# A planner's costs recalibrated, and the 64 sample rows stacked on TensorE

## The chip, the core and the metric

One core of a Trainium2 chip runs the whole program. The metric is device time in microseconds (us), the median of several executions. The kernel writes its instructions from Python; each engine (TensorE or PE, VectorE or DVE, ScalarE or ACT, GpSimd or POOL, and SP, which issues the DMAs) runs its own queue in order, and semaphores tie the queues together.

## The reference

One layer of a streaming encoder, applied to a prompt of 2048 rows and to a sample of 64 rows that continues a stream with 4096 past positions:

```python
h = rmsnorm(x, norm_g) @ w_in                     # 1024 -> 6144 columns
qa, ka, va, za, qb, kb, vb, zb, ga, gb = split(h)
# branch A: 4 heads, two softmaxes each over 64-wide halves of q and k, ALiBi, chunk-causal
a = softmax(s[0]) - lam * softmax(s[1]);  oa = a @ v
# branch B: chunkwise retention with a decaying state, 4 heads
oa = rmsnorm(oa, subln_g) * 0.2 * silu(za);  ob = rmsnorm(ob) * silu(zb)
y  = x + (sigmoid(ga) * (oa @ w_o_diff) + sigmoid(gb) * (ob @ w_o_ret)) @ w_out
```

All of it is float32. The sample's attention reads a cache of 4096 keys and values besides its own 64. The keys, values and retention states are outputs too.

## The kernel before

**Three products for one.** Most matmul operands are split into a high and a low part (`xh`, `xl` for the normalised input, `wh`, `wl` for a weight, a type that TensorE takes in one pass), and a product is the sum of high*high, high*low and low*high: three matmuls into one PSUM tile. ScalarE makes the high part by a cast, and VectorE or GpSimd makes the low part by a subtraction.

**Three streams of work.** `w_stream` is the input projection, in two halves of the prompt; the sample rides with the first half. `natural` and `opening` put x rows on the output's partitions (q, k, v), in tiles of 128 rows, and the ninth tile has the sample's 64 rows; `transposed` puts weight columns on the partitions instead. `z_stream` is attention and retention (`qk_block`, `softmax`, `at_pv`, `sample_attn`, `sample_pv`, `ret_block`). `out_stream` is the two output projections (`m_tile`, then `y_tile` for each 128 rows). `mm_group` issues the three matmuls for each of 8 chunks of 128 input columns.

**What sets the order.** Every task is a Python generator. The planner keeps one modelled clock per engine: `P`, `A`, `V` and `G` advance that of PE, ACT, DVE and POOL by an estimated cost and return when the result should be ready; `ld` and `st` do so for DMAs. A task yields the time it waits for, and the loop runs the first task in order of priority whose time is not after the modelled PE clock. The instructions of PE, ACT and DVE then stand in their queues in the order in which the Python code issued them; the order on SP and POOL is set by the framework. So these costs change no instruction, but they do change what stands ahead of what:

```python
def A(self, n, ready=0.0, extra=0.0):
    self.act = max(self.act, ready) + 0.84 * n + 165 + extra
    return self.act + LAT
```

**Places named later.** A projection result waits in an `mm` PSUM tile (two of them) until ScalarE copies it to an `ev` tile (three). `fin_qk` normalises q and k and transposes them on PE (`tp<-ident,raw`), `ret_block` does that for retention (`tp<-ident,rru`); both go through `rsqrt_small`, three VectorE operations on a handful of columns (`sm_t`, `sm_y`). `sample_attn` runs eight exponentials per head, and then `sample_pv` brings the two 64-row softmaxes together by DMAs across partitions (`both`, `s_num`, `s_den`). Weights are split by `wh<-ws` (ACT) and `wl<-ws,wh` (POOL). Line numbers in the profile of before are those of this listing.

Of the kernel before, what the change touches and what calls it, by code (L numbers as in the profile page):

```python
# [16 lines left out]
T = 2048  # L17
# [19 lines left out]
LAT = 250.0  # L37
DMA_LAT = 2600.0
# [22 lines left out]
class Hybrid:  # L61
# [78 lines left out]
    st = ld  # L140
# [26 lines left out]
    def consts(self):  # L167
        nc, i = self.nc, self.i
        cp = self.cp

        def c(name, shape, dt=F32):
            return cp.tile(shape, dt, tag=name, name=name)

        yield lambda: len(self.xt_ready) > 8
        self.fold = c("fold", [128, 64])
# [36 lines left out]
        nc.vector.tensor_scalar_add(lam, lam, 0.2)  # L212
        self.nlam = c("nlam", [128, 1])
        nc.vector.tensor_scalar_mul(self.nlam, lam, -1.0)
        self.lsam = c("lsam", [128, 1])
        nc.vector.memset(self.lsam[0:64, :], 1.0)
        nc.vector.tensor_copy(self.lsam[64:128, :], self.nlam[64:128, :])
        for _ in range(9):
            t = self.V(1)
        self.A(2)  # L220
        self.give("row", t)

    def rsqrt_small(self, ms, n, ready):
# [12 lines left out]
        for _ in range(3):  # L236
            self.tr = self.V(20, self.act)
# [86 lines left out]
    def norm_log(self, j):  # L324
        nc = self.nc
        ss, ms, y, t = self.xin[j][9:]
        nc.scalar.activation(y, ss, AF.Ln, scale=1.0 / D, bias=self.epst[:y.shape[0]])
        nc.scalar.activation(y, y, AF.Exp, scale=-0.5)
        self.A(1, 0, 40)
        self.xin[j].append(self.A(1, 0, 40))  # L330

    def norm_mean(self, j):
        ss, ms, y, t = self.xin[j][9:13]
        self.nc.vector.tensor_scalar(ms, ss, 1.0 / D, EPS, op0=ALU.mult, op1=ALU.add)
        self.V(1, t)

    def norm_root(self, j):
# [6 lines left out]
        for _ in range(3):  # L344
            self.V(20, t2)
# [23 lines left out]
    def x_tile(self, j, wait=True, mid=None):  # L369
# [6 lines left out]
        for q in range(2):  # L376
# [14 lines left out]
            self.give(tag, t2)  # L391
            if q == 0 and mid:
                yield from mid()
# [97 lines left out]
    def mm_group(self, ps, n, us, wsl, x, wfirst, last, between=None):  # L491
        nc = self.nc
        seg, xsl = x
        for c in range(KC):
# [3 lines left out]
            ops = ((a, xh), (a, xl), (b, xh)) if wfirst else ((xh, a), (xh, b), (xl, a))  # L498
            for i, (p, q) in enumerate(ops):
# [10 lines left out]
    def opening(self, fin):  # L510
# [5 lines left out]
        self.x_alloc(1)  # L516
        us, low = [], []
# [46 lines left out]
        for j in range(1, 9):  # L564
# [15 lines left out]
            ps = self.psum("mm")  # L580
# [3 lines left out]
            self.spawn(fin(ps[:r], r, 1, 128 * j if j < 8 else T, self.pe + LAT), 0, "w")  # L584
            yield self.pe

    def natural(self, half, fin, fresh=False, wide=False):
# [6 lines left out]
        for j0 in range(0, len(tiles), per):  # L594
# [3 lines left out]
            for u, (src, r, seg, col) in enumerate(group):  # L598
                if fresh:
                    yield lambda: len(self.xt_ready) > j0 + u  # L600
                    yield self.xt_ready[j0 + u]
                yield from self.mm_group(ps[:r, n * u:n * u + n], n, us, slice(0, n),
# [4 lines left out]
            self.spawn(fin(ps[:r, :n * len(group)], r, len(group), t0, self.pe + LAT), 0, "w")  # L607
            yield self.pe

# [6 lines left out]
    def fin_qk(self, which, g, nh=2):  # L616
# [4 lines left out]
        def fin(ps, r, nu, t0, t):  # L621
# [16 lines left out]
            self.give("mm", max(t1, t2))  # L638
# [10 lines left out]
            t = self.V(8)  # L649
# [3 lines left out]
            t = self.V(n)  # L653
# [42 lines left out]
    def fin_va(self, g, nh=2):  # L696
# [4 lines left out]
        def fin(ps, r, nu, t0, t):  # L701
# [13 lines left out]
            self.give("mm", max(t2, t3))  # L715
# [17 lines left out]
    def fin_vb(self, g):  # L733
# [3 lines left out]
        def fin(ps, r, nu, t0, t):  # L737
# [5 lines left out]
            self.give("mm", t)  # L743
# [50 lines left out]
    def rms_t(self, ps, n, gain, t, tag, tmp=None):  # L794
# [35 lines left out]
        self.A(n, t)  # L830
# [14 lines left out]
        else:  # L845
            yield t
            nc.vector.scalar_tensor_tensor(out=o, in0=o, scalar=gain, in1=y, op0=ALU.mult, op1=ALU.mult)
            t = self.V(n, t)
# [134 lines left out]
    def softmax(self, st, nk, b, pair):  # L983
# [4 lines left out]
        for units, mx, t in st:  # L988
# [11 lines left out]
        for c in range(2):  # L1000
            lsum = ls[c][:, 0:1]
            if len(rows[0]) > 1:
                lsum = sp.tile([128, 1], F32, tag="a_ls", name="a_ls")
                nc.vector.tensor_add(lsum, ls[c][:, 0:1], ls[c][:, 1:2])
                self.V(1, t)
            nc.vector.reciprocal(w[:, c:c + 1], lsum)
            self.V(1, t)
        nc.vector.tensor_mul(w[:, 1:2], w[:, 1:2], self.nlam)
        t = self.V(1, t)
        yield t  # L1010
        for k, (u0, u1) in enumerate(zip(rows[0], rows[1])):
            n = u0.shape[1]
            nc.scalar.activation(u1, u1, AF.Identity, scale=w[:, 1:2])  # L1013
            t1 = self.A(n, t, 90)
# [3 lines left out]
            t2 = self.V(n, t1)  # L1018
# [73 lines left out]
    def sample_attn(self):  # L1092
# [9 lines left out]
        for h in range(4):  # L1102
# [42 lines left out]
            for m in range(9):  # L1145
# [12 lines left out]
                if m < 8:  # L1158
# [3 lines left out]
                    t = self.V(512, t)  # L1162
# [19 lines left out]
            self.A(64, t, 220)  # L1182
            te = []
            for m in range(8):
                u = units[m // 2][:, (m % 2) * 512:(m % 2) * 512 + 512]
                nc.scalar.activation(u, u, AF.Exp, bias=mx[:, m:m + 1], scale=-1.0, accum_out=lp[:, m:m + 1])
                te.append(self.A(512, t, 220))
            self.spawn(self.sample_pv(h, units, both, tail, te, lp, oall), 2, "z")
# [4 lines left out]
        for h in range(4):  # L1193
            nc.tensor.matmul(fp[:, 64 * h:64 * h + 64], oall[:, 128 * h:128 * h + 128], self.fold,
# [29 lines left out]
    def v_split(self):  # L1224

        nc = self.nc
        for m in 4 * [*range(9)]:
# [11 lines left out]
            t = self.V(128 * nt, t)  # L1239
# [3 lines left out]
    def sample_pv(self, h, units, both, tail, te, lp, oall):  # L1243
# [7 lines left out]
        l, num, den = (sp.tile([128, 1], F32, tag=k, name=k, bufs=3) for k in ("s_l", "s_num", "s_den"))  # L1251
        nc.vector.tensor_reduce(l, lp[:, :9], axis=AX.X, op=ALU.add)
        nc.vector.tensor_copy(num[lo], l[lo])
        nc.vector.tensor_copy(den[up], l[up])
# [3 lines left out]
        self.ld(num[up], l[lo], 1 << 12)  # L1258
        t = self.ld(den[lo], l[up], 1 << 12)
        tt = sp.tile([64, 64], F32, tag="s_tt", name="s_tt", bufs=2)  # L1260
        self.ld(tt, tail[up], 1 << 14)
        for k in range(2):
            self.ld(both[k][lo], units[k][up], 1 << 18)
            t = self.ld(both[k][up], units[2 + k][lo], 1 << 18)
        yield t + 600
        nc.vector.reciprocal(den, den)
        nc.vector.scalar_tensor_tensor(out=den, in0=num, scalar=den, in1=self.nlam, op0=ALU.mult, op1=ALU.mult)
        nc.vector.reciprocal(num, num)
        for _ in range(3):
            self.V(1, t)  # L1270
        tb = []
        for k in range(2):
# [3 lines left out]
            self.V(1024)  # L1276
            nc.vector.scalar_tensor_tensor(out=b[up], in0=units[2 + k][up], scalar=den[up], in1=b[up],
                                           op0=ALU.mult, op1=ALU.add)
            tb.append(self.V(1024))
            self.give("row", tb[-1], 2)  # L1280
            yield self.pe
# [70 lines left out]
    def ret_block(self, k, t0, r, first):  # L1352
# [90 lines left out]
        t = self.V(8)  # L1443
# [3 lines left out]
        t = self.V(512, t2)  # L1447
# [47 lines left out]
    def split_fin(self, tag, h, l, s, t, on_pool, slot, key):  # L1495
# [8 lines left out]
        else:  # L1504
            yield t
            nc.vector.tensor_sub(l, s, h.bitcast(F32))
            t = self.V(n, t)
# [62 lines left out]
    def og_fin(self, on, z, t, og):  # L1570
# [9 lines left out]
        t = self.V(GW, t)  # L1580
# [10 lines left out]
        t = self.V(GW, t)  # L1591
# [3 lines left out]
    def gate(self, n, pair, tag):  # L1595
# [4 lines left out]
        for br in range(2):  # L1600
            self.nc.scalar.activation(pair[br], pair[br], AF.Sigmoid, bias=self.bg[:, br, ct:ct + 1])
            t = self.A(GW, t, 90)
# [38 lines left out]
    def m_fin(self, g, ct, pss):  # L1641
# [25 lines left out]
        for d, m in zip(self.ms, (h, l)):  # L1667
            nc.vector.tensor_copy(d[:, ct, 8 * g:8 * g + 8], m[:, 256:GW])
            t2 = self.V(8)
        self.msn.append(t2)  # L1670

    def y_tile(self, g, sel, r, x, y):
# [3 lines left out]
        for nh in range(2):  # L1676
            nsl = slice(512 * nh, 512 * nh + 512)
            yield from self.take("xt")
            xt = self.sb(pb, [128, 512], "xt", "oxt")[:r]
            tx = self.ld(xt, x[:, nsl], 2048 * r)  # L1680
            yield from self.take("at")
            run.append((nsl, xt, tx, self.psum("at")[:r]))
        first = 8 if sel is None else 7
        order = [(c, k) for k in range(2) for c in range(first)] + [(c, k) for c in range(first, 8) for k in range(2)]
        for ct, nh in order:
            nsl, xt, tx, ps = run[nh]
            yield lambda: len(self.wout) > ct and nh in self.wout[ct][2] and len(self.mq[g]) > ct
            h, l, t = self.mq[g][ct]
            if sel is None:
                yield lambda: len(self.msn) == 64  # L1690
                t = max(t, self.msn[-1])
                h, l = self.ms[0][:, ct, :], self.ms[1][:, ct, :]
            else:
                h, l = sel(h), sel(l)
            wh, wl, tw = self.wout[ct]
            if max(t, tw[nh]) > self.pe:
                yield max(t, tw[nh])
            nc.tensor.matmul(ps, h, wh[:, nsl], start=ct == 0, stop=False)  # L1698
            nc.tensor.matmul(ps, h, wl[:, nsl], start=False, stop=False)  # L1699
            nc.tensor.matmul(ps, l, wh[:, nsl], start=False, stop=ct == 7)  # L1700
            for _ in range(3):
                t = self.P(512)
            yield self.pe
            if ct == 7:
                self.spawn(self.y_fin(ps, xt, y[:, nsl], r, max(t, tx)), 0)
# [13 lines left out]
    def out_stream(self):  # L1719
# [4 lines left out]
        for g in range(8):  # L1724
# [3 lines left out]
            for tt in range(2):  # L1728
                t0 = 256 * g + 128 * tt
# [4 lines left out]
        yield from self.y_tile(7, None, 64, self.i["x_sample"][0], self.o["y_sample"][0])  # L1734

    def w_stream(self):
# [54 lines left out]
        self.ms = [self.z4.tile([128, 8, 64], F32R, tag=f"ms{j}", name=f"ms{j}") for j in range(2)]  # L1791
# [87 lines left out]
def const_arrays():  # L1879
    c = {}  # L1880
    c["c_ident"] = np.eye(128, dtype=np.float32)
    c["c_fold"] = np.concatenate([np.eye(64), np.eye(64)]).astype(np.float32)
# [49 lines left out]
```

## Time and profile before

| | |
|---|---|
| median of three executions | 1988.08 us (1986.14 to 1988.54) |
| profiled execution | 1990.07 us, of which its span is 1988.3 us |
| granted TensorE clock | 0.999 |
| busy: PE, PE weight load | 1963.8 us (99%), 1754.7 us (88%) |
| busy: DVE, ACT, POOL | 1057.2 us (53%), 991.0 us (50%), 417.3 us (21%) |
| DMA | 285.21 MB, mean 143 GB/s |

The busy time of PE counts every moment in which a matmul is under way. Matmuls are pipelined, so what one costs in a row of equals is the distance between two starts, which the timeline shows, and not its own duration.

### The profile page before, as it was taken

The numbers are of one execution on the slowest core, as the hardware profiler recorded it, in microseconds if no ns is written. First come the engines' busy times: TensorE is split into PE (matmuls) and PEld (weight loads), VectorE is DVE, ScalarE is ACT, GpSimd is POOL, SyncE is SP. The second block draws the span as 40 slices with busy tenths as digits, with TensorE's granted clock in tenths as the row PEclk, the third lists the DMA queues.
The fourth block names the chain that finished last, engine by engine and source line by source line (L and its number), as shares of the span: only waits on it lengthen the run. The fifth ranks groups of instructions, "written<-read, shape, count | busy, mean of one in ns | idle before, by whom it ended". The sixth has DMA issues, their size and how long they took to land.

```text
span 1988.3 us, 34106 instructions
## 1 busy us (share of the span) xinstructions
PE 1963.8 (99%) x12206; PEld 1754.7 (88%) x12206; DVE 1057.2 (53%) x2786; ACT 991.0 (50%) x2185; POOL 417.3 (21%) x383
## 2 busy tenths in 40 slices
PE   9999999999999999999999999999999999999999
PEld 7778989998998989999998888888888888889997
DVE  6453665446565326547756656525644356444432
ACT  6432666655454436436757656635744544333330
POOL 2310121212121221221111111211122434222210
PEclk9999999999999999999999999999999999999999
DMA  7646553335665756664352342652233666444431
GB/s 245 200 143 177 138 157 118 117 87 152 174 174 152 174 151 196 200 187 137 102 153 81 109 137 62 175 146 85 70 98 114 202 219 206 141 130 148 131 93 53
DMA packets 332508, 285.21 MB, mean 143 GB/s; under 512 B 65905, under 2 KB 297329, under 8 KB 332338
## 3 DMA queue, kind: packets, MB, share of 16 engines
q1 hardware_dynamic: 332338, 283.03, 48.5%
q8 instruction: 96, 1.57, 0.3%
q14 instruction: 74, 0.61, 0.1%
HBM read 187.19 MB, written 91.49 MB: 140 GB/s over the span
## 4 chain that ended last, share of the span: by engine, by line
PE 64%; DVE 2%; DMA 2%; ACT 1%; issue 0%; POOL 0%; SPq 0%; POOLq 0%; ACTq 0%; DVEq 0%
PE mm L500 31%; PE at L1698 3%; PE at L1699 3%; PE at L1700 3%; PE s L956 2%; PE s L957 2%; PE at L1063 2%; PE mm L1630 2%; PE s L1632 2%; PE mm L1631 2%; PE mm L1632 2%; PE s L1631 2%; PE s L1630 2%; PE pv L1043 1%; PE pv L1042 1%; PE pv L1041 1%
## 5 line engine op out<-in xcount | busy, mean ns | idle before, releaser
L500 PE MATMUL mm<-xh,wh 128*128 128x512 f32 (+2 forms) x1280 | 459.3, 359 | 2.8 <-ACT ev L770 2.8
L500 PE MATMUL mm<-xh,wl 128*128 128x512 f32 (+2 forms) x1280 | 452.4, 353 | 0.0
L500 PE MATMUL mm<-xl,wh 128*128 128x512 f32 (+2 forms) x1280 | 451.8, 353 | 0.0
L472 POOL TENSOR_TENSOR wl<-ws,wh 128x512 fp32r<-128x512 f32 x189 | 258.6, 1381 | 867.2 <-ACT wh L462 605.5
L500 PE MATMUL mm<-wh,xh 128*128 128x256 f32 (+3 forms) x864 | 273.5, 317 | 0.3 <-DVE tlo L713 0.3
L500 PEld LDWEIGHTS mm<-xh,wh 128*128 128x128 f32 x1280 | 241.4, 189 | 32.4 <-ACT ev L770 3.3
L500 PEld LDWEIGHTS mm<-xh,wl 128*128 128x128 f32 x1280 | 241.1, 188 | 31.9 <-POOL wl L472 0.4
L500 PE MATMUL mm<-wh,xl 128*128 128x256 f32 (+3 forms) x864 | 267.9, 310 | 0.1
L500 PE MATMUL mm<-wl,xh 128*128 128x256 f32 (+3 forms) x864 | 267.6, 310 | 0.0
L500 PEld LDWEIGHTS mm<-xl,wh 128*128 128x128 f32 x1280 | 241.6, 189 | 27.8
L1078 DVE TENSOR_TENSOR atl<-at,ath 128x512 fp32r<-128x512 f32 (+1 forms) x144 | 93.9, 660 | 159.2 <-ACT ath L1076 159.2
L500 PEld LDWEIGHTS mm<-wh,xh 128*128 128x128 f32 (+1 forms) x864 | 162.8, 188 | 11.8 <-PE s L957 0.4
L500 PEld LDWEIGHTS mm<-wl,xh 128*128 128x128 f32 (+1 forms) x864 | 162.9, 189 | 11.0
L500 PEld LDWEIGHTS mm<-wh,xl 128*128 128x128 f32 (+1 forms) x864 | 162.8, 188 | 10.9 <-DVE xl L389 0.6
L770 ACT COPY ev<-mm 128x512 f32<-128x512 f32 x140 | 71.3, 510 | 191.4 <-PE mm L500 166.4
L995 ACT ACTIVATE row<-row,a_mx 128x1024 f32<-128x1024 f32 (+7 forms) x160 | 153.3, 962 | 17.5 <-DVE a_mx L975 16.3
L965 DVE CUSTOM_DVE_ANT_0 row<-s,dfar 128x512 f32<-128x512 f32 (+2 forms) x192 | 118.2, 631 | 57.7 <-PE s L957 57.1
L462 ACT CAST wh<-ws 128x512 fp32r<-128x512 f32 x192 | 115.4, 618 | 33.2 <-PE mm L500 22.0
L1076 ACT CAST ath<-at 128x512 fp32r<-128x512 f32 (+1 forms) x144 | 78.6, 562 | 100.1 <-PE at L1063 95.2
L956 PE MATMUL s<-K,q 128*128 128x512 f32 (+3 forms) x320 | 118.3, 374 | 4.2 <-DVE a_acc L965 4.2
L957 PE MATMUL s<-K,q 128*128 128x512 f32 (+3 forms) x320 | 115.5, 362 | 0.0
L1016 DVE SCALAR_TENSOR_TENSOR row<-row,a_w 128x1024 f32<-128x1024 f32 (+4 forms) x96 | 102.6, 1074 | 21.5 <-ACT row L1013 21.4
(220 smaller groups left out, 3998.0 us busy)
## 6 DMA issues: line engine op xcount, KB each, us to landing
ws<-in_w_in_dram SPq DMA_DIRECT2D x192, 256.0 KB, 3.2
q<-qT SPq DMA_DIRECT2D x128, 128.0 KB, 3.0
V<-vN SPq DMA_DIRECT2D x24, 512.0 KB, 4.8
K<-kT SPq DMA_DIRECT2D x48, 256.0 KB, 4.1
gt<-gaT SPq DMA_DIRECT2D x64, 132.0 KB, 2.1
gt<-gbT SPq DMA_DIRECT2D x64, 132.0 KB, 2.1
xt<-in_x_prompt_dram SPq DMA_DIRECT2D x16, 512.0 KB, 5.9
kn<-in_cache_k_T_dram SPq DMA_DIRECT2D x32, 256.0 KB, 3.7
```

Of the source, the lines that this page charges most:

```text
L462: self.nc.scalar.copy(h, st)
L472: self.nc.gpsimd.tensor_sub(l, st, h.bitcast(F32))
L500: nc.tensor.matmul(ps, p, q, start=c == 0 and i == 0, stop=c == KC - 1 and i == 2)
L956: nc.tensor.matmul(ps, q1s, kk, start=True, stop=False)
L957: nc.tensor.matmul(ps, q2s, kk, start=False, stop=True)
L965: nc.vector.tensor_tensor_reduce(out=units[k0 // 1024][:, k0 % 1024:k0 % 1024 + n], in0=ps, in1=tab, scale=-SLOPES[h], scalar=3.0e38, op0= ...
L995: nc.scalar.activation(u, u, AF.Exp, bias=mx, scale=-1.0, accum_out=lp[:, k:k + 1])
L1016: nc.vector.scalar_tensor_tensor(out=u0, in0=u0, scalar=w[:, 0:1], in1=u1, op0=ALU.mult, op1=ALU.add)
L1078: nc.vector.tensor_sub(al[:, :w], at[:, :w], ah[:, :w].bitcast(F32))
L1630: nc.tensor.matmul(ps, wh[:, csl], oh, start=kt == 0, stop=False)
L1631: nc.tensor.matmul(ps, wh[:, csl], ol, start=False, stop=False)
L1632: nc.tensor.matmul(ps, wl[:, csl], oh, start=False, stop=kt == 3)
```

## The change

It has four parts.

1. **The sample's rows side by side.** For a tile of 64 rows, `xl` is put beside `xh` in a new tile `xs` (four POOL copies), so that one matmul with 128 stationary columns gives high*high on PSUM rows 0 to 63 and low*high on rows 64 to 127; high*low stays a matmul of its own. Three matmuls become two, in the projection (`mm_group`) and in the last product (`y_tile`, with `ms` as one tile). Afterwards the upper half has to come down: `halves` (copy on ACT, DMA, add on DVE) and `y_halves`. The sample's `y_tile` also moves ahead of the last prompt tile.
2. **The sample's softmax.** Each DMA into `both` is a task of its own (`s_move`) that follows its pair of exponentials; the sums of the two halves are folded by a small matmul with `fold` and not by two DMAs.
3. **Pacing.** `softmax` and `sample_attn` no longer queue all exponentials at once: after each the task sleeps until the modelled PE clock is within `PACE` of ACT's modelled clock. `sample_pv` does that on DVE.
4. **Costs.** Many estimates of `A` and `V` change, `SLACK` is added ahead of the transposes of `fin_qk` and `ret_block`, and a store no longer advances the modelled DMA clock.

The core of the diff (the other `V` and `A` costs change in the same way):

```diff
+SLACK = 400.0
+PACE = 700.0
-    st = ld
+    def st(self, dst, src, nbytes=0):
+        self.nc.sync.dma_start(dst, src)
+        return self.pe + nbytes / 150.0 + DMA_LAT
...
     def rsqrt_small
-            self.tr = self.V(20, self.act)
+            self.tr = self.V(70, self.act)
...
     def x_tile
+            if r == 64:
+                for k, part in enumerate((hi, lo)):
+                    nc.gpsimd.tensor_copy(self.xs[:, 4 * q:4 * q + 4, 64 * k:64 * k + 64], part)
+                    t2 = self.G(256, t2)
...
     def mm_group
+            if ps.shape[0] == 64:
+                pair = [(ps, xh, b), (both, self.xs[:, c, :], a)]
+                for i, (o, p, q) in enumerate(pair if c else pair[::-1]):
+                    nc.tensor.matmul(o, p, q, start=c == 0 and i == 0, stop=c == KC - 1 and i == 1)
+                    self.P(n)
+                ops = ()
...
+    def halves(self, ps, n, t, fin, t0):
+        yield from self.take("ev")
+        up = self.sb(self.ep, [128, 512], "ev", "up")[:, :n]
+        self.nc.scalar.copy(up, ps)
+        t = self.A(n, t)
+        self.give("mm", t)
+        yield t
+        yield from self.take("tlo")
+        dn = self.sb(self.ep, [128, 512], "tlo", "dn")[0:64, :n]
+        t = self.ld(dn, up[64:128], 256 * n)
+        yield t + 2000
+        self.nc.vector.tensor_add(up[0:64], up[0:64], dn)
+        t = self.V(n, t)
+        self.give("tlo", t)
+        yield from fin(up[0:64], 64, 1, t0, t, "ev")
...
     def fin_qk
-            t = self.V(8)
+            t = self.V(80)
...
-            t = self.V(n)
+            t = self.V(n + 100) + SLACK
...
     def softmax
-                t = self.A(u.shape[1], t, 220)
+                t = self.A(u.shape[1], t, 122)
+                yield self.act - PACE
...
-                self.V(1, t)
+                self.V(60, t)
...
     def sample_attn
-                te.append(self.A(512, t, 220))
+                te.append(self.A(512, t, 114))
+                if m % 2:
+                    lo, up = slice(0, 64), slice(64, 128)
+                    a, b = (lo, up) if m < 4 else (up, lo)
+                    self.spawn(self.s_move(both[m // 2 % 2][a], units[m // 2][b], te[-1], moved), 0, "z")
+                yield self.act - PACE
...
     def sample_pv
-        self.ld(num[up], l[lo], 1 << 12)
-        t = self.ld(den[lo], l[up], 1 << 12)
+        nc.tensor.matmul(ps[:, 0:2], self.fold, l, start=True, stop=True)
...
     def y_tile
+                pair = [(ps[:64], self.ms[:, ct, 0], wl[:, nsl]), (ps, self.ms[:, ct], wh[:, nsl])]
...
     def out_stream
+                if g == 7 and tt:
+                    yield from self.y_tile(7, None, 64, self.i["x_sample"][0], self.o["y_sample"][0])
-        yield from self.y_tile(7, None, 64, self.i["x_sample"][0], self.o["y_sample"][0])
```

**On PE, the sample's tile of the first projection.** Before, each chunk has three matmuls with 64 stationary columns (64 rows of output):

```order
L500 MATMUL mm<-wh,xl_117 128x512
L500 MATMUL mm<-wh,xh_116 64x512
L500 MATMUL mm<-wl,xh_116 64x512
L500 MATMUL mm<-wh,xl_117 64x512
L500 MATMUL mm<-wh,xh_116 64x512
L500 MATMUL mm<-wl,xh_116 64x512
```

Now it has two, and the first reads `xs`, which POOL has just written:

```order
L516 MATMUL mm<-wh,xl_117 128x512
L512 MATMUL mm<-wh,xs 128x512
L512 MATMUL mm<-wl,xh_116 64x512 x2
L512 MATMUL mm<-wh,xs 128x512
L512 MATMUL mm<-wl,xh_116 64x512
L512 MATMUL mm<-wh,xs 128x512
```

Eight chunks of three became eight chunks of two; before and behind them nothing moved.

**On ACT, the sample's exponentials of head 0** (`row,s_lp<-row,s_mx`), with the copies that free PE's PSUM tiles (`ev<-mm`). Before:

```order
L770 COPY ev<-mm 128x512
L1181 ACTIVATE s_tail,s_lp<-s_tail,s_mx 128x64
L1186 ACTIVATE row,s_lp<-row,s_mx 128x512 x8
L1235 CAST vhl<-vc 128x4x128
L827 ACTIVATE r_y<-tp,epst 128x256
L828 ACTIVATE r_y<-r_y 128x256
L829 ACTIVATE r_sq<-r_y 128x256
L770 COPY ev<-mm 128x256
```

Now:

```order
L1222 ACTIVATE s_tail,s_lp<-s_tail,s_mx 128x64
L1229 ACTIVATE row,s_lp<-row,s_mx 128x512
L1283 CAST vhl<-vc 128x4x128
L867 ACTIVATE r_y<-tp,epst 128x256
L868 ACTIVATE r_y<-r_y 128x256
L869 ACTIVATE r_sq<-r_y 128x256
L1229 ACTIVATE row,s_lp<-row,s_mx 128x512
L810 COPY ev<-mm 128x256
L470 CAST wh<-ws 128x512
L1229 ACTIVATE row,s_lp<-row,s_mx 128x512
```

The next copy of a PSUM tile stood behind eight exponentials and stands behind two.

More of the change, by code (lines that the diff above doesn't have):

```diff
@@ L1193, in sample_attn @@
         for h in range(4):
-            nc.tensor.matmul(fp[:, 64 * h:64 * h + 64], oall[:, 128 * h:128 * h + 128], self.fold,
+            nc.tensor.matmul(fp[:, 64 * h:64 * h + 64], oall[:, 128 * h:128 * h + 128], self.fold[:, :64],
                              start=True, stop=True)
@@ L1250, in sample_pv @@
         yield te[-1]
[L1251 to L1254, printed above, removed]
+        l = sp.tile([128, 2], F32, tag="s_l", name="s_l", bufs=3)
+        num, den = (sp.tile([128, 1], F32, tag=k, name=k, bufs=3) for k in ("s_num", "s_den"))
+        nc.vector.memset(l, 0.0)
+        nc.vector.tensor_reduce(l[lo, 0:1], lp[lo, :9], axis=AX.X, op=ALU.add)
+        nc.vector.tensor_reduce(l[up, 1:2], lp[up, :9], axis=AX.X, op=ALU.add)
         for _ in range(3):
@@ L1257, in sample_pv @@
         yield t
-        self.ld(num[up], l[lo], 1 << 12)
-        t = self.ld(den[lo], l[up], 1 << 12)
[L1260 to L1268, printed above, removed]
+        yield from self.take("s")
+        ps = self.psum("s")
+        nc.tensor.matmul(ps[:, 0:2], self.fold, l, start=True, stop=True)
+        t = self.P(512)
+        yield t
+        nc.vector.reciprocal(den, ps[:, 1:2])
+        nc.vector.reciprocal(num, ps[:, 0:1])
+        nc.vector.scalar_tensor_tensor(out=den, in0=ps[:, 0:1], scalar=den, in1=self.nlam,
+                                       op0=ALU.mult, op1=ALU.mult)
         for _ in range(3):
-            self.V(1, t)
+            t = self.V(100, t)
+        self.give("s", t)
+        yield lambda: len(moved) == 5
+        yield moved[-1] + 600
         tb = []
@@ L1691, in y_tile, with y_halves @@
                 t = max(t, self.msn[-1])
-                h, l = self.ms[0][:, ct, :], self.ms[1][:, ct, :]
+            if max(t, tw[nh]) > self.pe:
+                yield max(t, tw[nh])
+            if sel is None:
+                pair = [(ps[:64], self.ms[:, ct, 0], wl[:, nsl]), (ps, self.ms[:, ct], wh[:, nsl])]
+                for i, (o, m, w) in enumerate(pair if ct else pair[::-1]):
+                    nc.tensor.matmul(o, m, w, start=ct == 0 and i == 0, stop=ct == 7 and i == 1)
+                    t = self.P(512)
             else:
                 h, l = sel(h), sel(l)
[L1695 to L1702, printed above, removed]
+                nc.tensor.matmul(ps, h, wh[:, nsl], start=ct == 0, stop=False)
+                nc.tensor.matmul(ps, h, wl[:, nsl], start=False, stop=False)
+                nc.tensor.matmul(ps, l, wh[:, nsl], start=False, stop=ct == 7)
+                for _ in range(3):
+                    t = self.P(512)
             yield self.pe
             if ct == 7:
-                self.spawn(self.y_fin(ps, xt, y[:, nsl], r, max(t, tx)), 0)
+                self.spawn((self.y_fin if r == 128 else self.y_halves)(ps, xt, y[:, nsl], r, max(t, tx)), 0)
+    def y_halves(self, ps, xt, y, r, t):
+        nc = self.nc
+        yield from self.take("wst")
+        yt = self.sb(self.z4, [128, 512], "wst", "oyt")
+        yield t
+        nc.vector.tensor_copy(yt[64:128], ps[64:128])
+        t2 = self.V(512, t)
+        nc.vector.tensor_add(xt, ps[0:64], xt)
+        t = self.V(512, t)
+        self.give("at", t)
+        yield t2
+        t2 = self.ld(yt[0:64], yt[64:128], 1 << 17)
+        yield t2
+        nc.vector.tensor_add(yt[0:64], yt[0:64], xt)
+        t = self.V(512, max(t, t2))
+        self.give("wst", t)
+        yield t
+        self.give("wst", self.st(y, yt[0:64], 2048 * r))
     def y_fin(self, ps, xt, y, r, t):
@@ L1790, in w_stream @@
         self.z4 = self.es.enter_context(self.tc.tile_pool(name="p3b", bufs=1))
[L1791 removed]
+        self.ms = self.z4.tile([128, 8, 2, 64], F32R, tag="ms", name="ms")
         self.spawn(self.out_stream(), 8)
```

98 lines of the change are left out of this document (57 added, 41 removed).

## The prediction

> **What bounds the kernel now.** I read the page's first part and its chain first, then who PE waited for, then the places of those waits in the timeline. The chain's row gives shares of the span by engine.
>
> ```profile
> PE 1963.8 (99%) x12206; PEld 1754.7 (88%) x12206; DVE 1057.2 (53%) x2786; ACT 991.0 (50%) x2185; POOL 417.3 (21%) x383
> PE 64%; DVE 2%; DMA 2%; ACT 1%; issue 0%; POOL 0%; SPq 0%; POOLq 0%; ACTq 0%; DVEq 0%
> ```
>
> PE is the bound: it idles 1988.3 - 1963.8 = 24.5 us of the span, and no other engine passes 53%. Two things can therefore shorten the program: fewer matmuls, and fewer waits of PE. The waits between 30 and 1960 us, behind the start and ahead of the end (engine, line, what it waited for: total, times, longest):
>
> ```profile
> PE tp L1452 <- DVE rru L1446: 4.4, 3, 1.6
> PE s L956 <- DVE a_acc L965: 4.2, 6, 1.5
> PE mm L500 <- ACT ev L770: 2.8, 2, 2.2
> PE tp L667 <- ACT wh L462: 1.9, 1, 1.9
> PE tp L667 <- DVE raw L652: 0.9, 1, 0.9
> PE s L1375 <- DMA rqk<-kbT: 0.6, 1, 0.6
> PE at L1698 <- DVE oyt L1712: 0.4, 1, 0.4
> PE mm L500 <- DVE tlo L713: 0.3, 1, 0.3
> PE pv L1043 <- DVE atl L1078: 0.2, 1, 0.2
> ```
>
> They add up to 15.7 us. That is all a better order can give, and the matmuls of the sample are the rest.
>
> **Matmuls removed.** Counts by form, then starts of the sample's tile in the first projection (24 matmuls from 64.31 to 69.82), of a narrow one, of the sample's last product, and a row of the chain with 276 matmuls that have 128 stationary columns:
>
> ```profile
> L500 PE MATMUL mm<-wh,xl 128*64 128x512 f32 x24 | 9.4, 391 | 0.0
> L500 PE MATMUL mm<-wh,xl 128*64 128x256 f32 x16 | 4.4, 277 | 0.0
> L1699 PE MATMUL at<-wol,ms 128*64 128x512 f32 x16 | 6.3, 394 | 0.0
> 64.31 0.40 PE L500 MATMUL mm<-wh,xh 128*64 128x512 f32 x1
> ...
> 69.82 0.40 PE L500 MATMUL mm<-wh,xh 128*128 128x512 f32 x1
> 204.31 0.28 PE L500 MATMUL mm<-wh,xh 128*64 128x256 f32 x1
> ...
> 204.88 0.28 PE L500 MATMUL mm<-wh,xl 128*64 128x256 f32 x1
> 1973.19 0.45 PE L1698 MATMUL at<-woh,ms 128*64 128x512 f32 x1
> ...
> 1984.05 0.40 PE L1700 MATMUL at<-woh,ms 128*64 128x512 f32 x1
> 1542.53 62.62 PE mm L500 x276
> ```
>
> A 512-column matmul with 64 stationary columns costs 5.51 / 24 = 0.230 us, a 256-column one 0.57 / 5 = 0.114, one of the last product 10.86 / 47 = 0.231. With 128 stationary columns it is 62.62 / 276 = 0.227, so stacking `xl` on `xh` makes the surviving matmul no dearer. One matmul in three goes: 24 x 0.230 = 5.5, 16 x 0.114 = 1.8, 16 x 0.231 = 3.7, together 11.0 us. None of the waits above lies in these stretches, so all of it is on the path. [...]
>
> **Matmuls added.** Four `fold` matmuls, one per head. The nearest row is the other use of `fold`, whose four matmuls appear as eight passes:
>
> ```profile
> L1194 PE MATMUL pv<-fold,oall 128*128 128x64 f32 x8 | 1.0, 268 | 0.0
> ```
>
> I take its 1.0 us whole; with two columns and not 64 it could be less, between 0.5 and 1. It also waits for DVE's sums, but the planner gives PE other work there.
>
> **The stacked tile `xs`.** Four POOL copies of 128x256 stand between the sample's transposes and its first matmul at 64.31. The trace has no such copy; its nearest prices are a product of that size and a memset of twice the size:
>
> ```profile
> 58.12 3.78 POOL L472 TENSOR_TENSOR wl<-ws,wh 128x512 fp32r<-128x512 f32 x3 [4.99 <-DMA vN<-tlo]
> 62.01 0.41 DVE L389 TENSOR_TENSOR xl<-pv,xh 128x256 fp32r<-128x256 f32 x1
> L1370 POOL TENSOR_TENSOR rvx<-rqk,rtab 128x256 f32<-128x256 f32 x1 | 0.8, 750 | 11.1 <-DMA rqk<-qbT 11.1
> L278 POOL MEMSET gz<- 128x512 f32 x1 | 0.5, 525 | 0.3 <-POOLq L1917 0.3
> ```
>
> POOL is free at 61.90 and the last part is ready at 62.42. At 0.75 each the four end at 64.9, 0.6 late; at half the memset, 0.26, they end near 62.9 and hide. I take 0.3. It happens once.
>
> **What I cost at nothing.** `halves` adds five copies on ACT, five adds on DVE and five DMAs; they run beside matmuls on engines half busy, and the copy frees the `mm` tile sooner than `fin_va` or `fin_qk` did, which first collected their buffers. It holds an `ev` tile longer, which would bite only if three projection results came within one DMA; they come 5.5 us apart. The DMAs of `s_move` are those of before, issued earlier and one by one on SP; eight small DMAs go. `y_halves` has the whole last prompt tile for cover, 48 matmuls or 11 us. Behind the last matmul stand, as before, a DVE add and a store, now of 128 rows (KB each and us to landing):
>
> ```profile
> out_y_prompt_dram<-oyt SPq DMA_DIRECT2D x32, 256.0 KB, 2.4
> out_y_sample_dram<-oyt SPq DMA_DIRECT2D x2, 128.0 KB, 2.3
> ```
>
> That is 0.1 us.
>
> **The order.** Pacing has a clear case. ACT's eight exponentials of head 0 stand ahead of the copy that PE needs:
>
> ```profile
> 482.26 0.71 ACT L1186 ACTIVATE row<-row,s_mx 128x512 f32<-128x512 f32 x1
> ...
> 489.69 0.35 ACT L770 COPY ev<-mm 128x256 f32<-128x256 f32 x1
> 490.10 0.50 PE L500 MATMUL mm<-xh,wh 128*128 128x512 f32 x1 [2.24 <-ACT ev L770]
> ```
>
> In the new order that copy stands behind two of them; five fewer at about 0.7 each cover 2.24, and the other `ev` wait is of the same kind. I take 2.3 of the 2.8 as gone. The larger part has another cause. In retention's small VectorE operations:
>
> ```profile
> 802.75 0.16 DVE L233 SCALAR_TENSOR_TENSOR sm_t<-sm_y 128x4 f32<-128x4 f32 x1 [0.51 <-ACT sm_y L230]
> 802.76 1.31 POOL L1370 TENSOR_TENSOR rvx<-rqk,rtab 128x512 f32<-128x512 f32 x1 [12.11 <-PE mm L500]
> 802.95 1.15 DVE L234 TENSOR_TENSOR sm_t<-sm_t,ms 128x4 f32<-128x4 f32 x1
> 804.04 4.17 POOL L472 TENSOR_TENSOR wl<-ws,wh 128x512 fp32r<-128x512 f32 x3
> 804.13 1.20 DVE L235 SCALAR_TENSOR_TENSOR sm_y<-sm_t,sm_y 128x4 f32<-128x4 f32 x1
> 807.23 0.63 PE L1452 MATMUL tp<-ident,rru 128*128 128x128 f32 x4 [1.57 <-DVE rru L1446]
> ```
>
> An operation on four columns takes 0.16 us when POOL is idle and 1.15 to 1.20 while POOL subtracts, ending with POOL's instruction; so PE waited 1.57. The new costs put the transposes of `ret_block` and `fin_qk` later by 0.4 of `SLACK`, 3 x 0.05 in `rsqrt_small` and about 0.2 around it, some 0.75 us in all. That shortens each of the five waits of L1452 and L667 (7.2 us) by at most 0.75, 3.7 in all, if they fall as before. The softmax's small sums get 0.3 per block: about 1 of the 4.2 us on `s L956`. Against it, a new order makes new encounters of DVE with POOL, and at four retention blocks fewer matmuls now stand ahead of the transposes. I take 1.5 us as new waits of this kind, one of 1.57. Order: -2.3 - 3.7 - 1.0 + 1.5 = -5.5, and 1 us less for the encounters that I cannot place: -4.5. The ends are -13 (nearly all goes) and 0.
>
> **Sum.** -11.0 + 1.0 + 0.3 + 0.1 - 4.5 = -14.1 us. Against the profiled execution's 1990.07 that is 1976.0; that execution lies 2.0 above the median of 1988.08, so I predict 1974.0.
>
> **Rivals.**
> *The waits go nearly all.* For it: slack where PE waits, pacing where ACT is full. Against: the encounter above costs up to 1 us per operation, three in a row. 1988.1 - 9.6 - 13 = 1965.5. Chance 0.16.
> *The waits come back in full elsewhere.* A fixed slack cannot follow POOL, which the planner lets run unseen. Then only the matmuls count: 1988.1 - 9.6 = 1978.5, up to 1983 if some are added. Chance 0.24. [...]
> *Loads planned too early: not faster.* A store no longer advances the modelled DMA clock, so retention's loads are expected after 256 KB / 300 + 2600 ns = 3.5 us:
>
> ```profile
> rqk<-kbT SPq DMA_DIRECT2D x16, 256.0 KB, 4.7
> ```
>
> They take 4.7. If each of the 17 blocks made PE wait those 1.2 us, that is 20 us: 1988.1 - 9.6 + 20 = 1998.5. It cancels the matmuls from 0.6 us per block on. Against: only 0.6 us in all was lost to it before, with the same formula whenever the modelled queue was empty. Chance 0.07.
> *The halves cost what they save*, if PE waits for `xs` or an `ev` tile at all five sample groups, 2 us each: 1988. Chance 0.03.
>
> **Numbers.** The forecast has 0.50, between 1970 and 1977.5. The range of 8 in 10 runs from 1964 (the first rival's middle with 1.5 us more) to 1983 (the second's upper end). About 0.2%, 4 us, is what a measurement here can tell from no change: below 1984.1 is faster, 0.90, from the forecast and the first two rivals; the last two split into 0.05 and 0.05.
>
> **What would show it.** In the profile after: 56 fewer sample matmuls and PE busy down by about 10 us; no `ev` wait of 2 us beside a row of exponentials; `tp<-ident,rru` still among the waits, under 4.4; `xs` once, under 1. A new wait on `rqk` or `dn` would make the forecast wrong, and so would a middle sum of waits under 4 or over 15.

## The result and the profile after

The changed kernel takes 1972.25 us (median of five executions, 1969.46 to 1973.84), the kernel before 1988.54 on the same chip; the ratio is 0.9916, 95% interval 0.9904 to 0.9928, so 16.7 us less (16.3 by the two medians). The profiled execution took 1972.25 us, its span is 1970.5.

The busy time of the engines in the page after:

```profile
PE 1954.8 (99%) x12158; PEld 1753.9 (89%) x12158; DVE 1048.8 (53%) x2795; ACT 993.2 (50%) x2190; POOL 418.9 (21%) x387
```

PE is busy for 9.0 us less (1963.8 to 1954.8) and idle for 8.8 us less (24.5 to 1970.5 - 1954.8 = 15.7). Together that is the 17.8 us between the two spans. The first half is the matmuls, with a share of the clock that is worked out at the end; the second is the order. First PE's matmuls by shape (count, busy us, mean ns, idle before):

```profile
L512 PE MATMUL mm<-wh,xs 128*128 128x512 f32 x24 | 9.4, 394 | 0.0
L512 PE MATMUL mm<-wh,xs 128*128 128x256 f32 x16 | 4.0, 279 | 0.0
L1754 PE MATMUL at<-woh,ms 128*128 128x512 f32 x16 | 6.2, 398 | 0.1
L1313 PE MATMUL s<-s_l,fold 128*128 128x2 f32 x8 | 1.1, 208 | 0.0
```

The stacked matmuls wait for almost nothing, and each lasts as long as the narrow one did (394 ns beside 391). What one costs is the distance between starts. Here are the first start of the sample's tile and the next tile's, with 16 matmuls from one to the other where there were 24:

```profile
65.61 0.39 PE L512 MATMUL mm<-wh,xs 128*128 128x512 f32 x1
...
69.30 0.40 PE L516 MATMUL mm<-wh,xh 128*128 128x512 f32 x1
```

That is 3.69 / 16 = 0.231 us each; the tile took 5.51 us before, so one matmul in three is saved in full. Then who PE waited for between 30 and 1944 us (total, times, longest). Thirteen rows add up to 7.1 us, where nine added up to 15.7; five of 0.2 and one of 0.5 are left out here:

```profile
PE s L996 <- DVE a_acc L1005: 1.4, 2, 0.8
PE mm L516 <- DVE tlo L753: 1.0, 2, 0.9
PE s L1430 <- DMA rqk<-kbT: 0.8, 1, 0.8
PE at L1758 <- DVE oyt L1791: 0.8, 1, 0.8
PE pv L1349 <- DVE vhl L1286: 0.6, 1, 0.6
PE s L1685 <- DVE gt L1704: 0.6, 1, 0.6
...
PE s L997 <- DMA q<-qT: 0.4, 1, 0.4
...
```

The transposes (`tp`), 7.2 us of waits before, keep 0.2, and the `ev` copies, 2.8, are gone. The wait on `a_acc` fell from 4.2 to 1.4. The other places grew from 1.5 to 5.5, none longer than 0.9.

### The profile page after: what moved, and what is told of

It is laid out like the page before. It is cut to its first block, busy times and chain, and to the rows that moved or that the text cites. A ratio compares the mean times of both kernels' runs of the same rounds, so it can differ in the third digit from the quotient of the medians.

```text
span 1970.5 us, 34013 instructions
## 1 busy us (share of the span) xinstructions
PE 1954.8 (99%) x12158; PEld 1753.9 (89%) x12158; DVE 1048.8 (53%) x2795; ACT 993.2 (50%) x2190; POOL 418.9 (21%) x387
## 5 line engine op out<-in xcount | busy, mean ns | idle before, releaser
L516 PE MATMUL mm<-wh,xh 128*128 128x256 f32 (+1 forms) x824 | 258.4, 314 | 1.2 <-DVE tlo L753 1.0
L516 PE MATMUL mm<-wh,xl 128*128 128x256 f32 (+1 forms) x824 | 253.4, 308 | 0.0
L516 PE MATMUL mm<-wl,xh 128*128 128x256 f32 (+1 forms) x824 | 253.1, 307 | 0.1
L516 PEld LDWEIGHTS mm<-wh,xh 128*128 128x128 f32 x824 | 156.7, 190 | 10.9 <-DVE tlo L753 1.4
L516 PEld LDWEIGHTS mm<-wl,xh 128*128 128x128 f32 x824 | 156.9, 190 | 9.2 <-POOL wl L480 0.3
L516 PEld LDWEIGHTS mm<-wh,xl 128*128 128x128 f32 x824 | 156.7, 190 | 8.0
```

Of the source, the lines that this page charges most:

```text
L516: nc.tensor.matmul(ps, p, q, start=c == 0 and i == 0, stop=c == KC - 1 and i == 2)
```

## Experiments

Every ratio is to the kernel before, run beside it on the same chip. The runs lie on several chips, so differences between two changed kernels are read from their ratios.

### 1. Each half of the change alone

*The stacked rows alone* (part 1; parts 2 to 4 taken back, but for one cost of the copies into `ms`):

```diff
-    def st(self, dst, src, nbytes=0):
+    st = ld
...
-                yield self.act - PACE
...
-            t = self.V(n + 100) + SLACK
+            t = self.V(n)
```

> The stacked sample rows alone (xs, two matmuls for three, halves, y_halves, the sample's y_tile ahead of the last prompt tile); costs, pacing, slack, stores and the sample's softmax as before. If the matmuls are worth their distance between starts, PE's busy time falls by 11 us, its waits between 30 us and the end stay near 15.7 us, and the time is 11 us under before (ratio 0.9945). [...] If the halves make PE wait, it shows as new waits on up, dn, ev or xs and the gain is under 6 us.

Measured: 1975.88 us, ratio 0.9934 (0.9922 to 0.9946). PE's busy time is 1954.8, as after the whole change, and its waits sum to 11.7 us. So the matmuls are worth what the sum said, and the old costs, planned over 56 fewer matmuls, give an order with 4 us fewer waits by luck. Both kinds of wait are still there: `ev` 2.8, `tp` behind `wh` 1.9 and behind `rru` 1.8. (The profile names `wh`, which ended last. In the same wait of the kernel before, `raw`, which the transposes read, ended only 0.15 us ahead of them, at 982.55, behind three small VectorE operations of 1.27, 0.66 and 1.19 us.)

*The order alone* (parts 3 and 4 on the kernel before):

```diff
+SLACK = 400.0
+PACE = 700.0
...
-                t = self.A(u.shape[1], t, 220)
+                t = self.A(u.shape[1], t, 122)
+                yield self.act - PACE
```

> The planner's part alone (costs, SLACK, PACE, stores off the modelled DMA clock), three matmuls for the sample as before, its softmax as before. If the order gives its part by itself: PE busy as before (1964 us), waits down from 15.7 to about 7, time 7 to 9 us under before (ratio 0.9955 to 0.9965). If the order's gain is only there together with the new sample code, or by luck of one order, the waits stay over 11 us and the ratio is over 0.998.

Measured: 1979.05 us, ratio 0.9956 (0.9944 to 0.9968); the waits sum to 7.3 us, PE's busy time is 1963.1. The order therefore removes as many waits without the stacking as with it. The two halves, 13.1 and 8.8 us, add up to more than the 16.7 of the whole, and the likely reason is that 4 us of the stacking's 13.1 were waits that the order removes too.

### 2. Which part of the order

*Without the slack:*

```diff
-SLACK = 400.0
+SLACK = 0.0
```

> The changed kernel with SLACK at 0. Theory slack: the 0.4 us ahead of the transposes is what took the waits of tp<-ident,raw and tp<-ident,rru from 7.2 to 0.2 us, so 2 to 4 us of them come back, time 1974.5 to 1976. Rival, the measured costs or the new order did it: these waits stay under 1 us and the time within 1 us of 1972.3.

Measured: 1970.9 us, ratio 0.9910 (0.9897 to 0.9923), waits 8.8 us. One transpose waits for `raw`, 1.4 us, and none for `rru`. So the slack removed at most 1.4 of the 7.2 us. Its worth in time can't be told from nothing: the two intervals overlap, and in the profiled executions 1.7 us more of waits are set off by the opening, where this one had full clock and that of the changed kernel had not (last section).

*With the old small costs*, pacing and slack kept:

```diff
-            self.tr = self.V(70, self.act)
+            self.tr = self.V(20, self.act)
...
-                self.V(60, t)
+                self.V(1, t)
```

> The changed kernel with the many small estimates of VectorE and ScalarE put back (20 for 70, 8 for 80, 1 for 60 and so on), the slack, the pacing, the exponentials' costs and the store's rule kept. Theory A, the measured costs keep PE's tasks from being queued before their inputs are ready: the waits of the transposes on raw, wh and rru return, 3 to 7 us, and the time is 1975 to 1980. Rival B, pacing alone does it, and small costs only shuffle: the waits between 30 and 1944 us stay at 7 to 10 us and the time is 1970 to 1974. Rival C, the costs do harm elsewhere: below 1969.

Measured: 1977.91 us, ratio 0.9946 (0.9935 to 0.9958), waits 10.7 us, of which the first two rows:

```profile
PE pv L1082 <- ACT ath L1117: 2.3, 1, 2.3
PE tp L707 <- DVE raw L692: 1.7, 2, 0.9
```

The measured costs are worth about 6 us by the ratios. No wait on `rru` is back here either, and the largest wait is one that nobody expected, on `ath`: theory A holds for the time and, with 1.7 us on `raw`, in part for its mechanism.

*Without pacing* in `softmax` and `sample_attn`:

```diff
-                yield self.act - PACE
```

> The changed kernel without pacing on ACT: softmax and sample_attn queue all their exponentials at once, with the measured costs. Theory pacing: the waits mm<-ev come back with 2 to 3 us, one of 2 us beside eight exponentials of the sample; time 1974 to 1975.5. Rival, the measured cost of an exponential (114 in place of 220) already moves the copies right: no ev wait, time within 1 us of 1972.3.

Measured: 1985.48 us, ratio 0.9982 (0.9973 to 0.9990). Every expected time missed: pacing is worth 13 us, most of what the whole change gained, though the stacked rows are still in. (The `ev` waits came back with 2.7 us as expected, but none of 2 us.) The waits sum to 13.7 us; the first rows:

```profile
PE mm L516 <- ACT ev L810: 2.7, 2, 1.4
PE s L996 <- DVE a_acc L1005: 1.7, 3, 0.7
PE pv L1347 <- DVE vhl L1284: 1.6, 3, 1.2
PE s L1685 <- DVE w_o_retl L1559: 1.6, 1, 1.6
PE s L1683 <- ACT w_o_reth L1552: 1.5, 1, 1.5
```

Not only the `ev` copies are late but other work of ACT and DVE too, up to the last stage's weights. The waits alone do not make the 13 us: the profiled spans differ by 11.4 us, of which 6.6 are waits and 4.8 are PE's busy time (1959.6 beside 1954.8). Part of the 4.8 is clock. Behind waits near 480 and 1614 us this kernel has stretches of 3.4 us in which the granted clock was 0.50 and 0.52; in the changed kernel it was 1.00 from 476 to 500 and from 1600 to 1625. The rest was not traced.

*Pacing in the prompt's softmax only:*

```diff
     def sample_attn
-                yield self.act - PACE
```

> The changed kernel with pacing taken out of sample_attn alone; the prompt's softmax stays paced. Without both pacings it was 1985.5. Theory A, the eight sample exponentials ahead of the copy are what pacing cures (the prediction's reading of 482 to 490 us): the ev waits near 480 us return, about 2.7 us with a half-clock stretch of 1.7 behind them, and most of the 13 us, so 1978 to 1985. Rival B, it is the 17 blocks of prompt softmax per head pair, whose queued exponentials hold back everything ScalarE makes (wh, raw, w_o): here only the ev waits come back, 1974 to 1977. Rival C, either pacing suffices: 1971 to 1973.

Measured: 1979.21 us, ratio 0.9952 (0.994 to 0.9964), waits 12.5 us. So, taken out in this order, each of the two pacings gives about half: 1985.5 to 1979.2 for the softmax, to 1972.25 for the sample's eight exponentials. Theory A's mechanism stands in the timeline, at head 1 of the sample (start, duration, engine, line, what; in brackets PE's idle time and what ended it):

```profile
527.75 0.71 ACT L1229 ACTIVATE row<-row,s_mx 128x512 f32<-128x512 f32 x1
...
532.69 0.70 ACT L1229 ACTIVATE row<-row,s_mx 128x512 f32<-128x512 f32 x1
533.39 0.67 ACT L810 COPY ev<-mm 128x256 f32<-128x256 f32 x2
533.79 0.51 PE L516 MATMUL mm<-xh,wh 128*128 128x512 f32 x1 [2.79 <-ACT ev L810]
```

Eight exponentials stand ahead of the copy and PE waits 2.79 us for it. In the changed kernel five stand ahead of that copy at head 1 and three behind it, and PE waits for no `ev` copy. Its head 0 shows the copy and the weight's high part between the exponentials:

```profile
476.46 0.71 ACT L1229 ACTIVATE row<-row,s_mx 128x512 f32<-128x512 f32 x1
...
477.17 0.35 ACT L810 COPY ev<-mm 128x256 f32<-128x256 f32 x1
477.42 0.62 ACT L470 CAST wh<-ws 128x512 fp32r<-128x512 f32 x1
477.94 0.72 ACT L1229 ACTIVATE row<-row,s_mx 128x512 f32<-128x512 f32 x1
...
478.66 1.13 ACT L470 CAST wh<-ws 128x512 fp32r<-128x512 f32 x2
479.69 0.42 ACT L810 COPY ev<-mm 128x320 f32<-128x320 f32 x1
```

*A shorter pace:*

```diff
-PACE = 700.0
+PACE = 300.0
```

> The changed kernel with PACE 300 and not 700: the next exponential is queued later, closer to when ScalarE is free. If what counts is how little stands ahead of a new copy on ScalarE, fewer waits than 7.1 us and 1969 to 1972; if ScalarE now runs dry between exponentials and PE waits for the softmax instead (a_acc, atl, vhl, atp), slower, 1974 to 1982; if the exact value is without effect, 1971 to 1974.

Measured: 1966.93 us, ratio 0.9893 (0.9880 to 0.9906), waits 4.6 us, below what the first theory asked. This is the fastest version found, by one constant; its interval and the changed kernel's (0.9904 to 0.9928) just overlap, so the gain of about 5 us on the changed kernel is likely but not certain. Half of its waits is one place, the weights of the last stage:

```profile
PE s L1687 <- DVE w_o_retl L1561: 1.2, 1, 1.2
PE s L1685 <- ACT w_o_reth L1554: 1.2, 1, 1.2
```

### 3. GpSimd beside VectorE

The prediction laid the transposes' waits to VectorE's small operations being held up by GpSimd's subtractions. This kernel is the one before with all 189 of them moved to VectorE. The planner then charges them to VectorE's modelled clock, so the order can move a little too:

```diff
     def w_low
-        if n in (5, 7, 8):
+        if n:
             self.nc.vector.tensor_sub(l, st, h.bitcast(F32))
```

> The kernel before with nearly all weight subtractions wl moved from GpSimd to VectorE (189 of 128x512, 1.3 us each on GpSimd). Theory A, VectorE's small operations were held up by GpSimd (1.15 to 1.20 us beside 0.16): the operations of rsqrt_small go back to a maximum near 0.2 us, the waits on L1452 and L667, 7.2 us, fall below 3, and the time is 1982 to 1987 unless VectorE's own load makes new waits. Rival B, the small operations are slow for another reason (a queue behind something on VectorE): their maximum stays above 1 us and the waits stay; the time is 1988 or more.

Measured: 1974.9 us, ratio 0.9932 (0.9919 to 0.9945), better than theory A asked. Here the three operations of `rsqrt_small`, 51 of each, in the groups of before, of after, and of this kernel (busy us, mean ns of one):

```profile
L233 DVE SCALAR_TENSOR_TENSOR sm_t<-sm_y 128x8 f32<-128x8 f32 (+3 forms) x51 | 18.3, 358 | 19.6 <-ACT sm_y L230 19.6
L234 DVE TENSOR_TENSOR sm_t<-sm_t,ms 128x8 f32<-128x8 f32 (+3 forms) x51 | 15.1, 296 | 1.8
L235 DVE SCALAR_TENSOR_TENSOR sm_y<-sm_t,sm_y 128x8 f32<-128x8 f32 (+3 forms) x51 | 14.5, 285 | 1.7
```

```profile
L237 DVE SCALAR_TENSOR_TENSOR sm_t<-sm_y 128x8 f32<-128x8 f32 (+3 forms) x51 | 10.4, 203 | 19.1 <-ACT sm_y L234 19.0
L238 DVE TENSOR_TENSOR sm_t<-sm_t,ms 128x8 f32<-128x8 f32 (+3 forms) x51 | 10.5, 206 | 1.8
L239 DVE SCALAR_TENSOR_TENSOR sm_y<-sm_t,sm_y 128x8 f32<-128x8 f32 (+3 forms) x51 | 10.6, 208 | 1.7
```

```profile
L233 DVE SCALAR_TENSOR_TENSOR sm_t<-sm_y 128x8 f32<-128x8 f32 (+3 forms) x51 | 8.4, 164 | 10.4 <-ACT sm_y L230 10.4
L234 DVE TENSOR_TENSOR sm_t<-sm_t,ms 128x8 f32<-128x8 f32 (+3 forms) x51 | 8.4, 165 | 1.8
L235 DVE SCALAR_TENSOR_TENSOR sm_y<-sm_t,sm_y 128x8 f32<-128x8 f32 (+3 forms) x51 | 8.4, 165 | 1.7
```

Without GpSimd's subtractions an operation takes 165 ns on average; the same work costs 47.9 us before, 25.2 here, so 22.7 us of VectorE's time went to being held up. At the place that the prediction read (802.95 us in the kernel before: 1.15 us, and later 1.72 for the product on `rru`), this kernel has:

```profile
800.85 0.16 DVE L234 TENSOR_TENSOR sm_t<-sm_t,ms 128x4 f32<-128x4 f32 x1
...
801.25 0.69 DVE L1446 TENSOR_TENSOR rru<-rru,sm_y 128x512 f32<-128x512 f32 x1
```

So a larger operation is held up as well, 1.72 us beside 0.69. All of PE's waits in the middle that are left, 3.9 us of 15.7:

```profile
PE mm L500 <- ACT ev L770: 1.4, 2, 1.0
PE s L956 <- DVE a_acc L965: 0.8, 3, 0.3
PE mm L500 <- ACT wh L462: 0.7, 1, 0.7
PE s L1632 <- DVE w_o_retl L1506: 0.4, 1, 0.4
PE tp L1452 <- DVE rru L1446: 0.3, 1, 0.3
PE mm L500 <- DVE tlo L713: 0.3, 1, 0.3
```

This is shown: VectorE's small operations are held up (285 to 358 ns on average in the kernel before, 164 to 165 with the subtractions moved), and moving the subtractions takes away the transposes' waits, here and on the stacked rows below. It is not the subtraction as such: the first block in the prediction's rows ends with a product of retention (`rvx`, 802.76 to 804.07 us), and in a kernel below with the subtractions moved (PACE 100) one operation still took 1.27 us, from 798.40, beside such a product of 1.28 us from 798.37. The middle fence shows something that the prediction had not seen: in the changed kernel the subtractions are still on GpSimd (418.9 us busy), yet the small operations cost 31.5 us, so the new order loses far less to such encounters, by 16.4 us.

Three kernels then put this edit on other orders.

*On the stacked rows alone:*

```diff
-        if n in (5, 7, 8):
+        if n:
```

> The stacked rows alone (part 1, old costs, no pacing), with the weight subtractions moved from GpSimd to VectorE. Theory A, the new order cures mainly what GpSimd does to VectorE's small operations, and moving the subtractions cures it at the root: the 11.7 us of waits fall to 3 to 5 as they did in the kernel before (15.7 to 3.9), and the time is 1961 to 1966, below the changed kernel though it has none of its new order. Rival B, the kernel before was lucky in its order: the waits come back (8 us or more), 1968 to 1974.

Measured: 1969.51 us, ratio 0.9905 (0.9889 to 0.992), about 6 us below the stacked rows without it. The waits of the transposes are gone, but 9.7 us in all stay: 4.2 on `ev`, and 2.8 on DVE's parts of the last weights. Both numbers are in rival B's ranges, so the 3.9 us that this edit left in the kernel before owe something to luck in its order. Moving the subtractions cures the encounters, not the exponentials.

*On the changed kernel without pacing*, the same line:

> The changed kernel without pacing in softmax and sample_attn (1985.5 with subtractions on GpSimd), and with them on VectorE. Theory A, what pacing cures is exponentials ahead of a copy on ScalarE, whoever subtracts: the ev waits near 480 us stay (2.5 us or more) and the time stays above 1974. Rival B, without pacing the plan merely pushes VectorE's small operations into GpSimd's subtractions: waits fall to 3 to 5 us and the time is 1962 to 1967, pacing being worth little once the subtractions are gone.

Measured: 1990.66 us, ratio 1.0013 (1.0004 to 1.0022), waits 20.6 us. The time is on theory A's side and rival B is out, but not by the mechanism of theory A: of the `ev` waits (2.3 us) only 0.5 lie near 480 us, and the largest wait is one of the last stage that nobody expected:

```profile
PE mm L1683 <- ACT w_o_diffh L1552: 8.8, 1, 8.8
```

*On the changed kernel with a shorter pace, 300 and then 100,* the same line of `w_low` with:

```diff
-PACE = 700.0
+PACE = 300.0
```

> The changed kernel with both edits that gained so far: PACE 300 (1966.9) and the weight subtractions on VectorE. If the two cure different waits: those left fall from 4.6 to 1 to 3 us, 1962 to 1965. If the new order had already cured what GpSimd did, no gain: 1966 to 1968. If VectorE's 61 us more of work now holds up the paced softmax: above 1968.

Measured: 1977.21 us, ratio 0.9943 (0.9931 to 0.9956): the edit that gave the kernel before 13 us costs the fastest version 10. Its waits sum to 11.5, 6.9 more; the largest, 3.1, is in the last stage, and behind it the granted clock was 0.50 from 1604.0 to 1610.8 us.

> As the kernel before it in this set, with PACE 100: ScalarE gets its next exponential only when the model has it almost free. If less queued is always better, 1961 to 1964 and at or below PACE 300; if ScalarE now runs dry and PE waits for the softmax (atl, vhl, a_acc), 1966 to 1975.

Measured: 1975.09 us, ratio 0.9930 (0.9917 to 0.9944). The time lies at the upper end of the range expected for an ACT that runs dry, but the mechanism is not there: of the waits named for it only 0.2 us on `atl` appears. The largest wait is again on `w_o_diffh`, 4.2 us. The first loads of the last stage's weights, with PACE 300 and subtractions on GpSimd, then on VectorE (nanoseconds of one issue, then first and last start):

```profile
L138 SPq DMA_DIRECT2D wst<-in_w_o_diff_dram x16: 327/368/439, 1544.5 to 1594.0; - x16
```

```profile
L138 SPq DMA_DIRECT2D wst<-in_w_o_diff_dram x16: 328/382/1597, 1557.3 to 1603.2; - x16
```

They start 13 us later, and PE then waits 3.1 us for `w_o_diffh`. About 6 of the 13 are lateness of the whole kernel by then (PE's last `mm<-xh,wh` of the input projection starts at 1580.5 and at 1586.6). Why the plan puts the loads later still was not tried, so that stays open. On the order of the kernel before, the same edit moved their start from 1547.0 to 1543.7, while the last `mm<-xh,wh` moved from 1604.3 to 1588.7.

## Why the prediction was right, and where it was off

- **Matmuls, -11.0, and fold, +1.0.** Right. The stacked matmul is no dearer (0.231 us from start to start beside 0.230), and `fold` measures 1.1 us, together -9.9. PE's busy time fell by 9.0. The difference is clock, by the estimates of the last section: the opening lost 2.3 us after, and the 1.4 us that a stretch near 984 us lost before is gone.
- **`xs`, +0.3.** Nothing waits for it. The four copies took 0.40 us each on POOL, between the two bounds of 0.26 and 0.75.
- **`halves`, the tail, early loads.** No wait on `dn` appears, and `rqk` stays a single wait of 0.8 (0.6 before). The third and fourth rivals are out.
- **The order, -4.5: the mis-sized term.** PE's idle time fell by 8.8 us, the waits in the middle by 8.6, from 15.7 to 7.1. By places these are -2.8 for `ev` (forecast -2.3), -7.0 for the transposes (-3.7), -2.8 for the softmax's small sums (-1.0) and +4.0 for new waits (+1.5, and 1 more that could not be placed). Three terms were too small, and the new waits were dearer than forecast and in other places. For `ev` the place was right but pacing was undervalued: without it the time is 13 us higher, since work of ACT and DVE far from the copies comes late too. (The prediction counted five exponentials fewer ahead of the copy; from eight to two it is six.) For the transposes the credit went to the slack and the costs. The slack removed at most 1.4 us; the costs are worth 6 us in time. The new encounters that the +1.5 stood for did not come: the small operations lost 22.7 us to GpSimd before and 31.5 - 25.2 = 6.3 after. What exactly removed the waits on `rru` stays open, since slack, costs and pacing, each taken out alone, all leave them gone; the new costs of the exponentials and the rule for stores were not taken out alone.
- **The first rival** (nearly all waits go) was not met, with 7.1 us left; the shorter pace came close to it, with 4.6 us and 1966.93.
- **The second rival** (waits come back in full) had it right that the waits hang on POOL: taking its subtractions away took the transposes' waits with them (7.2 to 0.3). It did not follow that a new order must meet it as often.
- **What would show it.** The forecast that `tp<-ident,rru` stays among the waits holds in name only (0.2 us, L1507); the others (PE's busy time, no `ev` wait of 2 us, a sum between 4 and 15) held.

## What to carry to other kernels

Where an in-order engine serves both a long batch and a small copy that the bottleneck waits for, do not queue the batch at once: letting the exponentials in one after another as the queue empties was worth 13 us here, and a shorter pace about 5 more. The one wait that shows the batch is not the price of it: here it was 2.24 us. Small operations whose duration jumps sevenfold (0.16 to 1.15 us) were a sign of another engine here, not of their own cost; compare the group's mean with its minimum. A gain measured under one order is not a property of the edit: moving the subtractions gave 13 us on one order and cost 10 on another, so try such edits again after each change of the plan.

## What the runs showed of the hardware

After some waits of PE the granted clock fell to one half (0.50 to 0.52) for 3.4 us, which the page counts as busy time. Stretches of the kernel before around the wait of 1.88 us on L667 (window, length, then PE, PE's weight load, DVE, ACT and POOL busy with their instructions; PE's clock is the third number from the end):

```profile
980.00:983.60 3.60, 1.72 (x15) 1.55 (x15) 3.53 (x7) 2.89 (x6) 2.67 (x3) 1.00 0.39 115
983.60:987.00 3.40, 3.40 (x18) 3.40 (x17) 3.11 (x7) 3.40 (x7) 0.42 (x1) 0.51 0.59 184
987.00:990.00 3.00, 3.00 (x27) 3.00 (x26) 1.12 (x3) 1.51 (x3) 1.29 (x1) 0.99 0.39 134
```

At the later rate 3.4 us hold 30 matmuls, and 18 ran: 12 x 0.12 = 1.4 us lost, so by this estimate the wait of 1.88 cost 3.3. The kernel with pacing in the softmax only shows the same behind its 2.79 us for `ev` (0.50), and the opening of the changed kernel shows 6.8 us of it, where the same kernel without slack had full clock (0.50 beside 1.00):

```profile
535.20:538.60 3.40, 3.40 (x11) 2.72 (x10) 2.18 (x5) 0.00 (x0) 0.00 (x0) 0.50 1.02 217
```

```profile
10.80:17.60 6.80, 6.10 (x18) 4.84 (x18) 6.70 (x9) 3.90 (x9) 6.57 (x5) 0.50 1.04 412
```

```profile
10.90:17.70 6.80, 6.10 (x28) 4.11 (x27) 6.70 (x9) 6.21 (x14) 6.65 (x5) 1.00 1.03 412
```

Ten matmuls of 0.23 us fewer: by this estimate 2.3 us of PE's busy time after are the opening's clock. The two waits of PE near the start of these 6.8 us are nearly the same, 1.29 and 0.70 us after, 1.44 and 0.70 without slack, so like waits can meet either clock. Nor does the length alone decide: the wait of 1.88 us was followed by a clock of 0.51, the longer one of 2.24 us at 490 before by 1.00.

```profile
492.00:496.00 4.00, 4.00 (x18) 2.98 (x18) 3.94 (x4) 0.00 (x0) 4.00 (x3) 1.00 0.88 205
```

Which waits are hit was not tested by an experiment of its own, and how far it is chance can't be told from one profiled execution of each kernel.
